# Twelve gates as Strassen pairs, convolution projections inside attention, and the projections in a third plan

## The chip, the core and the metric

The kernel runs on one core of one Trainium2 chip. Time is device time in microseconds (us) of one launch. Each kernel is run several times on the chip, and the median is given; a profile is taken of one execution. Engines: PE (TensorE) does matmuls, ACT (ScalarE), DVE (VectorE) and POOL (GpSimd) do elementwise work, SP (SyncE) issues most DMAs.

## What is computed

One decoder block over 1024 tokens with 16 learned tokens in front. The input is normalised and projected to eight groups of 1024 channels. A gated short convolution and stick-breaking attention run on them side by side, each is projected again and weighted by a sigmoid gate; the sum is projected, normalised and added. A gated MLP with a convolution follows. Cut to what the change touches:

```python
    h = xn @ w_in
    b_c, c_c, h_c, q, k, v, g_conv, g_attn = jnp.split(h, list(splits), axis=-1)
    y_conv = b_c * causal_dwconv(c_c * h_c, conv_w_mix)
    branch_conv = y_conv @ w_proj_conv
    o = stick_breaking_attention(q.reshape(hd), k.reshape(hd), v.reshape(hd))
    branch_attn = o.reshape(bsz, seq_len, D_ATTN) @ w_proj_attn
    gate_conv = jax.nn.sigmoid(g_conv + b_gate[0])
    gate_attn = jax.nn.sigmoid(g_attn + b_gate[1])
    merged = gate_conv * branch_conv + gate_attn * branch_attn
    return merged @ w_out
```

Attention of one head takes, for each block of queries, the scores z, `sigmoid(-z)` (the chance that the stick doesn't break there), a running product of it from the newest key back, and the product of the result with differences of v.

## The kernel before

All float32 matmuls are done in three: each operand is split into a high part (rounded to float32r, a cast on ACT) and a low part (a subtraction on DVE or POOL), and high x high, high x low and low x high are summed in PSUM. 1026 columns (tokens) are kept of the 1040, in three chunks of 342 (`CH`).

A **plain block** makes 128 output channels: 8 row blocks of 128 inputs x 3 chunks x 3 matmuls, 72 matmuls of 342 columns (`plain`, `plain_step`, L356 to L358; in the later stage `Dense.run`, L256 to L258). A **Strassen pair** makes two blocks of 128 channels at once from seven products, each over half of the inputs and half of the tokens: 14 x 12 = 168 matmuls of 260 columns (`strassen_pair`, L807 to L810). It needs sums and differences of the weights (DVE, POOL), and of the tokens (`tops`, made once).

The stages that the change touches, in order of time:

1. **First stage** (`Plan` number one). xnT, the normalised input with channels on the partitions, high and low, stays in memory. Six blocks of q, k and v and one gate, the early one, are plain; the other 42 blocks (c, h, b of the convolution, then q, k, v) are 21 Strassen pairs. Their results are worked on (convolution, splits) and stored to DRAM: y_d, qh_d, ql_d, kh_d, kl_d, vv_d. A further plain gate, the bridge, closes the stage while the first head is loaded.
2. **Attention** (`Plan` number two). 16 heads (8 pairs p, two halves h), each in three units g. Per unit: scores on PE (z, L991 and L992), sigmoid on ACT (fl, L997), scan on DVE (fl, L1008), transposes on PE (tp, L1027), a cast on ACT (ah, L1032) and a subtraction on DVE (al, L458), then the product with v on PE (av, L1042 and L1043), two copies on ACT (L1065, L1068) and an add on POOL (L1072). After both halves POOL adds `ends` (L1085) and the 128 rows go to o_d. Twelve plain gates (`mid_gates`) are mixed in as fillers for PE; ACT evacuates them with Sigmoid (L682), and the gate goes to DRAM (gc_d, ga_d).
3. **Projections** (class `Dense`, in program order). Two late gates; eight blocks with w_proj_conv on y (loaded and split into yT by `load_split`), times the gate, to m_d (`item_pc`); eight blocks with w_proj_attn on the attention result (oT), times the gate, plus m_d (`item_pa`), to mb and mm_d. w_out is split meanwhile into w_o.
4. Output product (po, L1276 to L1278), normalisation, up-projection, down-projection.

In stages 1 and 2 the order on each engine is found ahead of time by class `Plan`: every task has an engine, a cost, a key (the time at which it should run), predecessors, and slots that it takes and frees (buffers, PSUM banks). The planner steps through time, gives each free engine the ready task with the lowest key whose slots are free, and emits it; the instructions of an engine are then held in that order. "ANY" means DVE or POOL, whichever comes first. A task in front that waits on the chip holds up all that stands behind it on its engine. PE thus takes a filler where no attention task is ready.

## Time and profile before

| | |
|---|---|
| median of 3 runs | 1978.43 us (1977.09 to 1979.53) |
| the profiled execution | 1979.65 us, span 1977.8 us |
| mean granted PE clock | 0.993 of full |
| busy: PE, DVE, ACT, POOL | 97%, 58%, 42%, 33% of the span |
| DRAM read, written | 166.02 MB, 70.46 MB |

A row of a group view reads: line, engine, operation, output and inputs, shapes, count, then busy us and mean ns of one, then idle time just before them and what ended it. A row of a window table reads: the window and its length, then for each engine its busy us and, in brackets, its instructions; then PE's granted clock, the share of the DMA engines that was busy, and GB/s. A row of a timeline reads: start, duration, engine, line, operation. PE and DVE instructions overlap at their ends, so a sum of means is somewhat above the busy time.

### The profile page before, as it was taken

What the parts mean: (1) busy time and instruction counts of PE and PEld (TensorE: products, weight loads), DVE (VectorE), ACT (ScalarE), POOL (GpSimd) and SP (SyncE); (2) the same over time, 40 slices, a digit from 0 to 9 for tenths busy, and PEclk for the clock granted to TensorE, in tenths of its full rate; (3) what the DMA queues carried; (4) which work ended last, traced back from release to release, by engine and by line L of the source; (5) the groups of instructions that cost most, each with busy time, mean ns of one, the idle gap of its engine ahead of it and who ended that gap; (6) DMA issues with size and microseconds to landing.
All of it is one profiled execution on the core that took longest, in us unless ns stands there. A gap on an engine that the chain in (4) does not pass through costs nothing.

```text
span 1977.8 us, 32044 instructions
## 1 busy us (share of the span) xinstructions
PE 1918.2 (97%) x12732; PEld 1805.0 (91%) x12732; DVE 1137.9 (58%) x1732; ACT 838.6 (42%) x1766; POOL 647.0 (33%) x484
## 2 busy tenths in 40 slices
PE   6999999999999999999999999889999999999997
PEld 6999999999989999998899999879889988888886
DVE  6836666665457888878331146864544444355547
ACT  5533333344447666767421223544443444321122
POOL 1110000000113232323134631256565555553363
PEclk9999999999999999999999999999999999999999
DMA  3522121454496444542575663221213121353224
GB/s 141 162 80 85 65 79 51 145 151 143 153 236 168 121 142 121 142 120 76 173 215 173 201 175 107 83 86 64 86 65 107 65 85 65 118 168 99 85 86 138
DMA packets 73841, 238.55 MB, mean 121 GB/s; under 512 B 15400, under 2 KB 17224, under 8 KB 72668
## 3 DMA queue, kind: packets, MB, share of 16 engines
q1 hardware_dynamic: 70368, 226.00, 37.6%
q10 hardware_dynamic: 3324, 10.50, 1.7%
q8 instruction: 100, 1.64, 0.3%
q14 instruction: 49, 0.40, 0.1%
HBM read 166.02 MB, written 70.46 MB: 120 GB/s over the span
## 4 chain that ended last, share of the span: by engine, by line
PE 82%; DVE 10%; ACT 2%; DMA 2%; issue 1%; POOL 1%; SPq 0%; ACTq 0%; DVEq 0%; POOLq 0%
PE st L807 7%; PE st L810 7%; PE st L809 7%; PE st L1429 7%; PE st L1431 6%; PE st L1433 6%; DVE fl L1008 4%; PE st L1723 3%; PE st L1721 3%; PE st L1722 3%; PE mm L256 3%; PE mm L257 3%; PE mm L258 3%; PE tp L1027 2%; PE mm L356 2%; PE mm L357 2%
## 5 line engine op out<-in xcount | busy, mean ns | idle before, releaser
L1008 DVE TENSOR_TENSOR_SCAN fl<-fl,upper 114x470 f32<-114x470 f32 (+3 forms) x144 | 208.9, 1466 | 29.9 <-ACT fl L997 29.3
L184 POOL TENSOR_TENSOR a_op<-raw,a_op 128x512 fp32r<-128x512 f32 (+1 forms) x136 | 194.0, 1440 | 88.6 <-ACT a_op L183 85.9
L807 PE MATMUL st<-tT,s_op 128*128 128x260 f32 x672 | 190.9, 284 | 0.0
L809 PE MATMUL st<-tT,s_op 128*128 128x260 f32 x672 | 190.1, 283 | 0.0
L810 PE MATMUL st<-tT,s_op 128*128 128x260 f32 x672 | 190.1, 283 | 0.0
L1429 PE MATMUL st<-opT,a_op 128*128 128x258 f32 (+2 forms) x528 | 171.3, 324 | 4.1 <-ACT snap L1444 1.9
L1431 PE MATMUL st<-opT,a_op 128*128 128x258 f32 (+2 forms) x528 | 169.3, 321 | 2.0 <-DVE opT L184 1.1
L1433 PE MATMUL st<-opT,a_op 128*128 128x258 f32 (+2 forms) x528 | 169.3, 321 | 0.0
L458 DVE TENSOR_TENSOR al<-tp,ah 114x342 fp32r<-114x342 f32 (+3 forms) x288 | 116.9, 442 | 62.5 <-ACT ah L1032 61.7
L183 ACT CAST a_op<-raw 128x512 fp32r<-128x512 f32 (+1 forms) x136 | 85.0, 634 | 155.8 <-DMA raw<-in_w_up_gate_dram 52.4
L1728 DVE TENSOR_TENSOR acc<-acc,st 128x512 f32<-128x512 f32 x144 | 98.5, 687 | 91.1 <-PE st L1723 91.1
L807 PE MATMUL st<-xnT,s_op 128*128 128x260 f32 x504 | 142.5, 283 | 0.0
L1032 ACT CAST ah<-tp 114x342 fp32r<-114x342 f32 (+3 forms) x288 | 106.5, 405 | 84.5 <-PE tp L1027 78.2
L810 PE MATMUL st<-xnT,s_op 128*128 128x260 f32 x504 | 142.3, 282 | 0.0
L809 PE MATMUL st<-xnT,s_op 128*128 128x260 f32 x504 | 141.9, 282 | 0.0
L187 DVE TENSOR_TENSOR raw<-raw 128x512 f32<-128x512 f32 x76 | 76.7, 1009 | 109.0 <-POOL a_op L184 107.0
L1072 POOL TENSOR_TENSOR ot<-ot,half 64x342 f32<-64x342 f32 x48 | 60.3, 1256 | 233.7 <-ACT ot L1068 233.6
L763 ACT CAST s_op<-raw 128x512 fp32r<-128x512 f32 x126 | 77.8, 621 | 124.1 <-PE st L810 116.1
L1431 PE MATMUL st<-opB,a_op 128*128 128x512 f32 (+2 forms) x396 | 127.4, 322 | 1.9 <-DVE opB L184 1.9
L1429 PE MATMUL st<-opB,a_op 128*128 128x512 f32 (+2 forms) x396 | 127.2, 321 | 0.0
L810 PEld LDWEIGHTS st<-tT,s_op 128*128 128x128 f32 x672 | 126.9, 189 | 0.0
L1433 PE MATMUL st<-opB,a_op 128*128 128x512 f32 (+2 forms) x396 | 126.8, 320 | 0.0
(221 smaller groups left out, 5891.0 us busy)
## 6 DMA issues: line engine op xcount, KB each, us to landing
raw<-in_w_in_dram SPq DMA_DIRECT2D x64, 512.0 KB, 3.4
raw<-in_w_up_gate_dram SPq DMA_DIRECT2D x44, 512.0 KB, 3.7
act_d<-owork SPq DMA_DIRECT2D x22, 512.0 KB, 4.2
araw<-act_d SPq DMA_DIRECT2D x22, 512.0 KB
raw<-in_w_down_dram SPq DMA_DIRECT2D x22, 512.0 KB, 3.6
qh<-qh_d SPq DMA_DIRECT2D x32, 256.5 KB, 5.9
ql<-ql_d SPq DMA_DIRECT2D x32, 256.5 KB, 6.6
vv_d<-vt SPq DMA_DIRECT2D x16, 512.0 KB, 3.6
```

The costliest lines, as they stand in the source:

```text
L183: nc.scalar.copy(hi, src)
L184: (lo_engine or nc.vector).tensor_tensor(lo, src, hi.bitcast(F32), op=ALU.subtract)
L458: eng.tensor_tensor(out, src, hi.bitcast(F32), op=ALU.subtract)
L807: nc.tensor.matmul(ps, wt[:, 0, c], xh, start=start and kb == 0, stop=False, skip_group_check=True)
L809: nc.tensor.matmul(ps, wt[:, 0, c], xl, start=False, stop=False, skip_group_check=True)
L810: nc.tensor.matmul(ps, wt[:, 1, c], xh, start=False, stop=kb == 3, skip_group_check=True)
L1008: nc.vector.tensor_tensor_scan(fl[:, ::-1], fl[:, ::-1], upper[:, NT - nk:][:, ::-1], 1.0, op0=ALU.mult, op1=ALU.max)
L1032: nc.scalar.copy(kst["ah"][:n, off:], kst["tp"][:n, off:CH])
L1429: nc.tensor.matmul(ps, wt[:, 0, k], xh, start=start and kb == 0, stop=False, skip_group_check=True)
L1431: nc.tensor.matmul(ps, wt[:, 0, k], xl, start=False, stop=False, skip_group_check=True)
L1433: nc.tensor.matmul(ps, wt[:, 1, k], xh, start=False, stop=stop and kb == 3, skip_group_check=True)
L1728: nc.vector.tensor_tensor(a, a, ps, op=ALU.add)
```

## The change

- Twelve of the 16 gates become six Strassen pairs at the end of the first stage. `done_gate` applies the Sigmoid in one ACT pass over 1026 columns and stores the gate.
- The attention stage gets two plain gates and six of the eight convolution projections as fillers. When the two gates have read xnT for the last time, its memory becomes yT (tag "xy"), and `split_rows` loads the eight row blocks of y into it in place and splits them. The projections' chunks are evacuated on DVE, times the gate (`conv_item`).
- Attention rows 0 to 5 are loaded and split during attention or right behind it into tiles that heads no longer use (`open_qk`, `open_vv`, `both_spare`); rows 6 and 7 into new tiles at the start of the third plan. The store of the last pair's rows is issued by ACT's queue, the others by SP's.
- The class `Dense` is gone. The last two convolution projections and the eight attention projections are tasks of a third `Plan`, which also loads and splits w_out (into the memory of yT once it is free). Most elementwise work there that was fixed to POOL or DVE is "ANY" now, and the order of each engine is held as in the other plans.
- Some later tiles change between the left and the right side of the memory.

```diff
-    xnT = xnt_pool.tile([P, 2, KB, NT], F32R, name="xnT")
+    xnT = xnt_pool.tile([P, 2, KB, NT], F32R, name="xnT", tag="xy")
-    gates = [(1, ob) for ob in range(8)] + [(0, ob) for ob in range(8)]
-    N_FIRST, N_LATE = 1, 2
-    early_gate, bridge_gate = gates[0], gates[1]
-    mid_gates = gates[2:16 - N_LATE]
-    late_gates = [ob for _, ob in gates[16 - N_LATE:]]
-
-    def load_raw(o):
+    gates = [(1, 0)] + [(0, ob) for ob in range(8)] + [(1, ob) for ob in range(1, 8)]
+    early_gate, bridge_gate, mid_gates = gates[0], gates[13], gates[14:]
+    N_LATE = 2
...
+    def plain(o, chunks, key, evac, finish, psum, first_chunk=0, given=None, w=w_in, src=src_x,
+              ready=(), eng="ANY", by="ACT", lead=16.0, space=("wk",), after=()):
+        st = raw_weights(o, w, key - lead) if given is None else given
+        if "hi" not in st and "los" not in st:
+            split_weights(st, key, eng)
+        los = st["los"]
+        before, evacs, banks = None, [], {}
...
+                                  (before, los[kb // 4] if los else None, ready[kb] if ready else None),
+                                  at, (plan_bank,) if kb == 0 else ())
+            evacs.append(plan.add(by, (act_cost if by == "ACT" else dve_cost)(n),
+                                  lambda ci=ci, a=a, n=n: evac(a, n, banks[ci], ci == first_chunk),
+                                  (before, *evacs[-1:], *after), at - 4,
+                                  space if ci == first_chunk and first_chunk == 0 else (), (plan_bank,)))
-        finish(evacs[-1:], at)
+        finish(evacs, at)
...
+    def done_gate(which):
+        def done(ob, u, after, key):
+            t = plan.add("ACT", act_cost(NQ), lambda: nc.scalar.activation(
+                u()[:, T0:], u()[:, T0:], AF.Sigmoid, bias=bias_gate(which, ob)), tuple(after), key + 3)
+            plan.add("SP", dma_cost(NQ), lambda: nc.sync.dma_start(
+                (gc_d, ga_d)[which][ob * P:(ob + 1) * P, :], u()[:, T0:]), (t,), key + 4, (), ("wk",))
+        return done
...
+    blocks += [(48 + 8 * which + ob, ob, done_gate(which)) for which, ob in gates[1:13]]
...
+    nxt = [split_weights(raw_weights(48 + 8 * which + ob, w_in, at - 20.0), at, "ANY")]
+    which, ob = mid_gates[1]
+    nxt.append(raw_weights(48 + 8 * which + ob, w_in, at))
...
-    plan = Plan({"raw": 2, "whi": 1, "wlo": 1, "mm": 2, "z": 2, "tp": 3, "av": 1, "qk": 2, "vv": 1,
+    plan = Plan({"raw": 1, "whi": 1, "wlo": 1, "mm": 2, "z": 2, "tp": 3, "av": 1, "qk": 2, "vv": 1,
...
-    whole_time = len(mid_gates) * item + 250.0
+    fillers = len(mid_gates) + KB - N_LATE
+    whole_time = fillers * item + 250.0
...
         fin = plan.add("POOL", pool_cost(NQ), last_add, tuple(ot_parts), t_o + 1)
-        plan.add("SP", dma_cost(NQ), lambda p=p: nc.sync.dma_start(o_d[p * P:(p + 1) * P, :], out_tiles[p][:, :NQ]),
-                 (fin,), t_o + 1, (), ("ot",))
+        q, cost = (nc.sync, dma_cost(NQ)) if p < NPAIR - 1 else (nc.scalar, 0.15)
+        plan.add("SP" if q is nc.sync else "ACT", cost, lambda p=p, q=q: q.dma_start(
+            o_d[p * P:(p + 1) * P, :], out_tiles[p][:, :NQ]), (fin,), t_o + 1, (), ("ot",))
...
+        evac, finish = gate_out(which, ob, work_tile, ("wk",))
+
+        def ended(evacs, key, finish=finish):
+            mid_last.extend(evacs)
+            finish(evacs, key)
+
+        plain(48 + 8 * which + ob, CH_Q, 20.0 * i, evac, ended, bank_mm, 0, nxt[i],
+              eng="POOL", lead=34.0)
+    def split_rows(kb, parts, src_d, key, after, begin=None, takes=()):
+        def load():
+            if begin is not None:
+                begin()
+            nc.sync.dma_start(parts()[1].bitcast(F32), src_d[kb * P:(kb + 1) * P, :])
+
+        def high():
+            nc.scalar.copy(parts()[0], parts()[1].bitcast(F32))
+
+        def lower(e):
+            hi, lo = parts()
+            low(engine_of(e), lo, lo.bitcast(F32), hi)
+
+        t = plan.add("SP", dma_cost(NQ), load, after, key, takes)
+        t = plan.add("ACT", act_cost(NQ), high, (t,), key)
+        return plan.add("ANY", any_cost(NQ), lower, (t,), key)
...
+    def open_y():
+        t = xnt_pool.tile([P, 2, KB, NT], F32R, name="yT", tag="xy")
+        for kb in range(KB):
+            feats["y", kb] = t[:, 0, kb, :NQ], t[:, 1, kb, :NQ]
...
+    def conv_item(ob, key, tile_of, psum, ready, given=None):
+        u = {}
...
+            g = u["g"][:, a:a + n]
+            nc.vector.tensor_tensor(g, g, ps, op=ALU.mult)
...
+        ld = plan.add("SP", dma_cost(NQ), load, (), key - 8, ("wk",))
+        plain(ob, CH3, key, evac, finish, psum, 0, given, w_proj_conv, src_of("y"), ready, "POOL", "DVE",
+              34.0, (), (ld,))
+    y_open = plan.add(None, 0.0, open_y, tuple(mid_last))
+    y_ready = [split_rows(kb, lambda kb=kb: feats["y", kb], y_d, 24.0 + 2.5 * kb, (y_open,))
+               for kb in range(KB)]
+    late_from = whole_time + 10.0
+    for ob in range(KB - N_LATE):
+        conv_item(ob, 50.0 + (whole_time - 30.0) * ob / (KB - N_LATE), work_tile, bank_mm, y_ready)
+    nxt = [split_weights(raw_weights(KB - N_LATE, w_proj_conv, late_from - 30.0), late_from, "POOL")]
+    nxt.append(raw_weights(KB - N_LATE + 1, w_proj_conv, late_from - 10.0))
...
+    for kb, begin, slot, at in ((0, open_qk, "qk", last_head), (1, open_vv, "vv", last_head + 1),
+                                (2, open_qk, "qk", last_head + 20), (4, open_qk, "qk", late_from),
+                                (5, open_vv, "vv", late_from + 1)):
+        o_ready[kb] = split_rows(kb, lambda kb=kb: feats["o", kb], o_d, at, (), begin(kb), (slot,))
...
-    items = [item_gate(0, ob) for ob in late_gates]
-    n_gates = len(items)
-    dense = Dense(psB0.enter_context(pool("ps_mmB", 3, space=PSUM)), items)
...
-    items += [item_pc(ob) for ob in range(8)] + [item_pa(ob) for ob in range(8)]
-    k = 0
-    for _ in range(24):
-        dense.chunk()
-        if k < 8:
-            load_split(oT, o_d, k)
-            k += 1
...
+    plan = Plan({"raw": 1, "whi": 1, "wlo": 1, "mm": 3, "wk": 2, "ld": 2}, plan)
+    nxt[0]["los"] = nxt[1]["load"] = None
+    o_ready = {kb: split_rows(kb, lambda kb=kb: feats["o", kb], o_d, 2.5 * kb - 15.0, ()) for kb in (6, 7)}
+    o_ready.update((kb, None) for kb in range(6))
+    for i in range(N_LATE):
+        conv_item(KB - N_LATE + i, item * i, lambda: sw_tile("gcl", "wk"), bank_b, (), nxt[i])
...
+    y_users = [t for t in plan.tasks if t.engine == "PE"][-1:]
+    for ob in range(KB):
+        attn_item(ob, item * (N_LATE + ob))
...
+    w_open = plan.add(None, 0.0, open_w, tuple(y_users))
+    for i in range(KB):
...
+        key = item * (N_LATE + 0.85 * i + 0.5)
+        t = plan.add("SP", dma_cost(D), load, (w_open,), key, ("raw",))
+        t = plan.add("ACT", act_cost(D), high, (t,), key + 5)
+        t = plan.add("ANY", any_cost(D), lower, (t,), key + 6)
```

The parts left out move `plain`'s loads into `raw_weights` and `split_weights`, put the attention projections into `attn_item` with the same arithmetic, and open the tiles named above.

More of the change, by code (lines that the diff above doesn't have):

```diff
@@ L914, in block_kernel @@
     at += item
-    nxt = {}
     which, ob = mid_gates[0]
-    def next_load():
-        nxt["raw"] = load_raw(48 + 8 * which + ob)
-    def next_high():
-        nxt["hi"], nxt["lo"] = whole(nxt["raw"])
-        nc.scalar.copy(nxt["hi"], nxt["raw"])
-    ld = plan.add("SP", dma_cost(D), next_load, (), at - 20, ("raw",))
-    h = plan.add("ACT", act_cost(D), next_high, (ld,), at - 10, ("whi", "wlo"))
-    plan.join([plan.add("ANY", any_cost(512),
-                        lambda e, j=j: lo_piece(nxt["raw"], nxt["hi"], nxt["lo"], j, e, 512),
-                        (h,), at - 9) for j in range(2)], ("raw",))
+    nxt = [split_weights(raw_weights(48 + 8 * which + ob, w_in, at - 20.0), at, "ANY")]
+    which, ob = mid_gates[1]
+    nxt.append(raw_weights(48 + 8 * which + ob, w_in, at))
     plan.run()
@@ new lines, in block_kernel, with open_qk, begin, open_vv @@
+    spare = []
+    def open_qk(kb):
+        def begin():
+            tiles = [heads["pool"].tile([P, n], F32R, name=t, tag=t)
+                     for t, n in (("qh", NQ), ("ql", NQ), ("kk", NT))]
+            feats["o", kb] = tiles[0], tiles[1]
+            spare.append(tiles[2][:, :NQ])
+        return begin
+    def open_vv(kb):
+        def begin():
+            v = values_tile().rearrange("p k h d -> p (k h d)")
+            feats["o", kb] = v[:, :NQ], v[:, 1152:1152 + NQ]
+        return begin
@@ L1114, in block_kernel @@
+    m_ctx = ctx.enter_context(ExitStack())
+    mpool = m_ctx.enter_context(pool("mblk", 2, "right"))
     s_ctx = ctx.enter_context(ExitStack())
     sw = s_ctx.enter_context(pool("sw", 2, "right"))
[L1116 to L1125 removed]
@@ L1220, in block_kernel, with bank_b, sw_tile @@
-    for i in range(24):
-        if i % 3 == 0:
-            load_wo(i // 3)
-        dense.chunk()
-        if i % 3 == 1:
-            split_wo(i // 3)
+    def bank_b():
+        return ps_mmB.tile([P, 512], F32, name="mm", tag="mm")
+    def sw_tile(name, tag):
+        return sw.tile([P, NT], F32, name=name, tag=tag)
+    plan = Plan({"raw": 1, "whi": 1, "wlo": 1, "mm": 3, "wk": 2, "ld": 2}, plan)
+    nxt[0]["los"] = nxt[1]["load"] = None
+    o_ready = {kb: split_rows(kb, lambda kb=kb: feats["o", kb], o_d, 2.5 * kb - 15.0, ()) for kb in (6, 7)}
@@ L1226, in block_kernel @@
+    plan.run()
+    pin_to = len(nc.cur_bb.bb.instructions)
     s_ctx.close()
-    slots_de.close()
+    heads_ctx.close()
     psB0.close()
```

352 lines of the change are left out of this document (118 added, 234 removed).

## The prediction

> **What bounds the kernel now.** I read the page's busy shares first, then the chain of waits, then windows by stage, because the mean hides stages with different limits.
>
> ```profile
> span 1977.8 us, 32044 instructions
> PE 1918.2 (97%) x12732; PEld 1805.0 (91%) x12732; DVE 1137.9 (58%) x1732; ACT 838.6 (42%) x1766; POOL 647.0 (33%) x484
> ...
> PE 82%; DVE 10%; ACT 2%; DMA 2%; issue 1%; POOL 1%; SPq 0%; ACTq 0%; DVEq 0%; POOLq 0%
> ```
>
> TensorE (PE) is the bound nearly everywhere; the chain passes through DVE for 10%, part of it in attention. The change touches three stretches, so I cut the span there: a steady piece of the first stage, attention, the gap behind it, and the projections.
>
> ```profile
> core 0: us, PE busy (x) PEld busy (x) DVE busy (x) ACT busy (x) POOL busy (x), PEclk, DMA share, GB/s
> 150.00:200.00 50.00, 50.00 (x420) 50.00 (x419) 33.00 (x48) 20.19 (x42) 2.58 (x2) 1.00 0.24 75
> 551.00:948.00 397.00, 385.07 (x2657) 364.11 (x2657) 312.14 (x432) 260.99 (x672) 111.99 (x84) 1.00 0.51 135
> 970.00:985.00 15.00, 11.80 (x52) 10.58 (x51) 7.40 (x16) 7.49 (x17) 2.77 (x4) 0.77 0.88 287
> 985.00:1155.00 170.00, 170.00 (x1087) 170.00 (x1086) 38.91 (x84) 35.60 (x62) 79.97 (x91) 1.00 0.66 197
> ...
> 551.00:948.00 397.00, 172.16 (x877) 139.69 (x878) 0.00 (x0) 19.68 (x36) 1.00 0.51 135
> ```
>
> The last row is the same window for the projection tiles (mm) alone. Four boundaries come from the timeline and the tile view of po:
>
> ```profile
> 551.47 0.22 PE L991 MATMUL z<-kk,qh 128*114 128x128 f32 x1
> ...
> 947.49 0.22 PE L1042 MATMUL av<-ah,vv 114*128 114x114 f32 x1
> 947.60 0.32 PE L1043 MATMUL av<-al,vv 114*128 114x114 f32 x1
> ...
> L1276 PE MATMUL po<-w_o,mb x216: 314/319/396, 1156.3 to 1262.7; 128*114 128x342 f32 x72, 128*114 128x340 f32 x36
> ```
>
> Attention runs from 551.5 to 947.9, 396.4 us; the projections end at 1156.3, 208.4 us later. In attention PE is 97% busy and DVE 79%; 877 of the 2657 matmuls are fillers, so PE is the bound only because gates are mixed in.
>
> **The first stage: plus 120.0 us.** A Strassen pair is 14 products of 12 matmuls, 168. The steady piece does 420 in 50 us, 119.0 ns each: 20.0 us a pair, six pairs 120.0. Two plain blocks are 144 matmuls at 170 / 1087 = 156.4 ns, 22.5 us. So the move saves 2.5 us of PE a pair, 15 in all. The pairs' other work (weight splits, two Sigmoid passes over 1026 columns) has cover: DVE is busy 33 of 50 us there and ACT 20, and PE never stops. Without that cover a Sigmoid would cost about what an ACT pass over 1026 columns does, quoted below, 1.2 us. Between full cover and 12 of those, I take nothing.
>
> **The projections: minus 95.8 us.** Behind the last av matmul only 720 matmuls remain before the output product: two convolution blocks and eight attention blocks, 720 x 156.4 ns = 112.6 us against 208.4. This also removes the stall behind attention: in the 15 us from 970 PE did 52 matmuls where 96 fit, at a granted clock of 0.77, because it waited for rows of y. Now y is long loaded; attention rows 6 and 7 take its place as the late input. Behind the last av stand two ACT copies, two POOL adds, the store (on ACT's queue, so ACT waits for POOL with the splits of row 5 and of the second convolution block's weights behind it), a load and a split. SP's queue is not held by that wait. By these rows the weights are split about 9 us behind the last av, row 7 about 15 (a load like the store's 4.2, a cast and a subtraction behind it):
>
> ```profile
> L1065 ACT COPY half<-av 64x342 f32<-64x342 f32 x48 | 21.1, 440 | 16.3 <-PE av L1043 15.7
> L1072 POOL TENSOR_TENSOR ot<-ot,half 64x342 f32<-64x342 f32 x48 | 60.3, 1256 | 233.7 <-ACT ot L1068 233.6
> L1085 POOL TENSOR_TENSOR ot<-ot,ends 128x1026 f32<-128x1026 f32 x8 | 15.2, 1902 | 0.6
> L380 POOL TENSOR_TENSOR wlo<-raw,whi 128x512 fp32r<-128x512 f32 x22 | 32.9, 1512 | 53.6 <-PE z L992 35.7 <-ACT whi L469 14.5 <-PE tp L1027 3.5
> L557 ACT CAST hi<-su 128x1026 fp32r<-128x1026 f32 x8 | 8.4, 1052 | 5.3 <-DVE su L831 5.2
> L526 ACT ACTIVATE su<-su,par 128x1026 f32<-128x1026 f32 x8 | 9.3, 1157 | 2.6 <-DVE su L523 2.6
> act_d<-owork SPq DMA_DIRECT2D x22, 512.0 KB, 4.2
> ```
>
> The weights are needed after one block (11.3 us), row 7 after two (22.5): I count nothing, at worst 5 us.
>
> **Attention: the term that decides.** Fillers fall from 875 to 576 matmuls, which would shorten a PE-bound stage by 299 x 156.4 ns = 46.8 us. PE's own need becomes 385.1 - 877 x 0.1564 = 247.9, plus 90.1, 338.0. But DVE's need grows: 18 gated evacuations leave ACT for DVE, and seven of the eight y splits fall to DVE.
>
> ```profile
> L1164 DVE TENSOR_TENSOR gcl<-gcl,mm 128x342 f32<-128x342 f32 x24 | 12.1, 509 | 49.6 <-PE mm L258 45.0 <-DMA gcl<-gc_d 4.6
> L458 DVE TENSOR_TENSOR su<-su,hi 128x1026 fp32r<-128x1026 f32 x8 | 9.8, 1226 | 7.8 <-ACT hi L557 7.8
> ```
>
> 18 x 0.509 + 7 x 1.226 = 17.7 us, so DVE needs 312.1 + 17.7 = 329.8. On DVE, inside attention before (al: low half of a transposed block, fl: scan):
>
> ```order
> L1008 SCALAR_TENSOR_TENSOR fl<-fl,upper 114x584
> L458 TENSOR_TENSOR al<-tp,ah 114x342 x2
> L1008 SCALAR_TENSOR_TENSOR fl<-fl,upper 114x698
> L458 TENSOR_TENSOR al<-tp,ah 114x342
> L458 TENSOR_TENSOR al<-tp,ah 114x228
> ```
>
> and now:
>
> ```order
> L900 SCALAR_TENSOR_TENSOR fl<-fl,upper 114x584
> L353 TENSOR_TENSOR al<-tp,ah 114x342
> L1041 TENSOR_TENSOR gt<-gt,mm 128x342
> L353 TENSOR_TENSOR al<-tp,ah 114x342 x2
> L900 SCALAR_TENSOR_TENSOR fl<-fl,upper 114x698
> L353 TENSOR_TENSOR al<-tp,ah 114x342
> ```
>
> An evacuation (gt) now stands between al's, behind PE's last product of its chunk, with al's and scans queued behind it.
>
> On PE, near the end before, late gates (L256 to L258) still filled in:
>
> ```order
> L1042 MATMUL av<-ah,vv 128x342
> L256 MATMUL mm<-xnT,whi 128x342
> L1043 MATMUL av<-al,vv 128x342
> L1027 MATMUL tp<-ident,fl 114x114
> L1042 MATMUL av<-ah,vv 128x342
> L257 MATMUL mm<-xnT,whi 128x342
> ```
>
> and now, the last three fillers:
>
> ```order
> L253 MATMUL mm<-yT,whi 128x342
> L254 MATMUL mm<-yT,whi 128x342
> L255 MATMUL mm<-yT,wlo 128x342
> L934 MATMUL av<-ah,vv 128x342
> L935 MATMUL av<-al,vv 128x342
> L883 MATMUL z<-kk,qh 114x242
> ```
>
> Behind these, 102 of the 576 av, 117 of the 720 transposes and 42 of the 480 z follow with nothing between them: more than two of the 16 heads run bare. How dense DVE gets is read from windows of attention:
>
> ```profile
> 552.00:576.00 24.00, 21.66 (x137) 19.77 (x137) 15.08 (x18) 11.64 (x30) 2.39 (x1) 1.00 1.04 224
> 576.00:936.00 360.00, 352.06 (x2444) 334.21 (x2442) 288.73 (x400) 242.90 (x626) 106.02 (x82) 1.00 0.48 132
> ...
> 564.00:576.00 12.00, 9.66 (x61) 7.83 (x60) 10.58 (x13) 7.72 (x21) 2.39 (x1) 1.00 1.04 199
> 636.00:648.00 12.00, 10.81 (x77) 9.90 (x74) 11.33 (x15) 8.54 (x24) 4.77 (x4) 1.00 0.25 74
> 732.00:744.00 12.00, 11.16 (x79) 10.51 (x78) 11.33 (x14) 8.72 (x25) 5.51 (x4) 1.00 0.15 47
> 924.00:936.00 12.00, 10.20 (x68) 8.45 (x66) 11.83 (x16) 9.52 (x25) 5.01 (x6) 1.00 0.33 111
> 936.00:948.00 12.00, 10.35 (x71) 9.13 (x72) 8.33 (x16) 6.12 (x17) 3.58 (x2) 1.00 0.06 25
> ```
>
> Start (24 us) and end (12 us) hold few scans and stay as they are, with half a us ahead of them. The middle holds 288.7 us of DVE work and gets 17.7 more: 306.4. DVE reaches 94% where it is pressed (11.33 of 12, twice) and 99% at 924, where fillers are nearly absent. At 94% the middle takes 326.0 us and attention 36.5 + 326.0 = 362.5, 33.9 less than before. The bounds: PE's 338.0 plus the 11.9 us it idles today, 350; or 88%, the pressed window at 564, 348.2 + 36.5 = 384.7. I take 94%, as two separate windows show it with PE at 90 and 93%.
>
> Behind the two gates y is loaded into the tile that held xnT, and five attention rows follow near the end: thirteen loads of half a megabyte on SP among the head loads, with the DMA share at 0.51 today. They have room. But PE's queue meets the first convolution matmuls before all rows of y are split, and a late row would block the transposes and scores behind it. Eight loads at the 4.2 us of the store above, one behind the other, take 34 us; the order puts some 55 z, 53 transposes and 40 av between the last gate matmul and the eighth row's, about 20 us on PE and 25 at DVE's pace. So the delay lies between nothing and 9 us; loads overlap, so I take nothing and keep 9 for the rivals.
>
> POOL's work there stays near 112 us: 14 weight pieces and six row splits, each as long as two pieces, for 30 pieces. But it meets denser scans:
>
> ```profile
> 560.94 1.38 DVE L1008 TENSOR_TENSOR_SCAN fl<-fl,upper 114x584 f32<-114x584 f32 x1 [1.64 <-ACT fl L997]
> ...
> 635.30 2.47 DVE L1008 TENSOR_TENSOR_SCAN fl<-fl,upper 114x584 f32<-114x584 f32 x1
> ...
> 635.25 3.58 POOL L380 TENSOR_TENSOR wlo<-raw,whi 128x512 fp32r<-128x512 f32 x2 [3.34 <-ACT whi L469]
> ```
>
> The same scan takes 1.38 us alone and 2.47 beside a pair of POOL's pieces. The mean over attention already holds such meetings, so by the rows alone I add nothing. The Trainium skill's page GPSIMD Engine Reference, section 1 Specifications, speaks against that: POOL shares its SBUF interfaces with VectorE, with contention where a DVE instruction has two SBUF inputs, so every meeting with a scan costs. By that rule, as an estimate, 15 pairs with scans on half the time are 8 meetings now, and 13 in a denser DVE at most 13: 5 x 1.1 = 5.5 us more, and the sum below would be -4.2 instead of -9.7. The trace shows the meeting; no run of before shows how many the new order makes.
>
> **The sum.** 120.0 - 95.8 - 33.9 = -9.7 us. Output product, up-projection and down-projection keep their instructions; their tiles change sides of the memory, which I count at nothing (plus or minus 2 us). The profiled execution took 1979.65 us, 1.85 over its span; it would take 1970.0. The median of the runs shown, 1978.43, is 1.2 lower: 1968.7.
>
> **Rivals.**
>
> *PE stays the bound.* DVE packs so well that only today's 11.9 us of PE idle remain: attention 350, 22 us gained, 1956. For it: 924 to 936. Against: bare heads, where the window at 936 keeps DVE at 69% and PE at 86%.
>
> *DVE does not pack: slower.* Place: the ring of transposes, ACT's casts and DVE's al. Its waits today:
>
> ```profile
> DVE al L458 <- ACT ah L1032: 61.7, 66, 3.4
> DVE fl L1008 <- ACT fl L997: 29.3, 31, 9.4
> ```
>
> 91 us of waiting; my forecast leaves DVE about 33. If the order with gt between al's and the bare heads holds DVE at 88%, attention takes 384.7, and the total is 1991. Below 90.2% it is slower by more than 4 us, above 92.4% faster by more than that. For it: the whole middle runs at 80% today. Against: there PE was the limit.
>
> *No change.* What is saved elsewhere goes back in attention: y rows 9 us late, five more meetings of a scan with POOL (2.47 against 1.38 us, 5.5 in all), or DVE at 91.3%, which makes attention 372.2 and the total 1978.4.
>
> **How the numbers follow.** A measurement here can tell 0.2%, 4 us, from no change. Forecast (attention 357 to 368) 0.42, PE-bound 0.16, no change 0.21, DVE not packing 0.17, a loss elsewhere 0.04 (a wait at the projections' start or the out product, 5 to 10 us). Faster is the first two, 0.58; slower 0.21. The forecast's own range is 1963 to 1974; with PE-bound at the low end and most of the no-pack case at the high end, 1956 to 1986 holds 8 in 10.
>
> **What would show it.** First stage: six more pairs at 420 matmuls per 50 us. Attention: about 362 us from first z to last av, DVE above 91%, its waits for ah below 40 us, PE idle some 25 us, most in the last 40 us. Projections: 112 to 113 us with no idle and a clock of 1.00. It is wrong if PE waits for yT, if DVE stays under 90%, or if the second late convolution block waits for its weights.

## The result and the profile after

The changed kernel takes 1966.26 us (median of four runs, 1964.59 to 1968.02), the kernel before beside it 1978.0; the ratio is 0.994, with an interval of 0.9923 to 0.9957. That is faster by 0.6%. The prediction was 1968.7.

The page of the changed kernel's profile:

```profile
span 1966.1 us, 32363 instructions
PE 1909.8 (97%) x12876; PEld 1793.0 (91%) x12876; DVE 1194.9 (61%) x1820; ACT 858.5 (44%) x1786; POOL 600.2 (31%) x404
```

The span is 11.7 us shorter than before. Windows cut it at the same places as the prediction: two pieces of the added Strassen pairs, attention, projections, output product.

```profile
core 0: us, PE busy (x) PEld busy (x) DVE busy (x) ACT busy (x) POOL busy (x), PEclk, DMA share, GB/s
550.00:600.00 50.00, 50.00 (x419) 50.00 (x418) 24.39 (x43) 21.04 (x39) 2.57 (x2) 1.00 0.29 96
600.00:660.00 60.00, 60.00 (x502) 60.00 (x502) 23.66 (x42) 23.71 (x45) 0.00 (x0) 1.00 0.38 106
672.00:1029.00 357.00, 344.61 (x2360) 319.51 (x2359) 318.26 (x457) 253.84 (x651) 119.71 (x76) 0.99 0.57 157
1029.00:1142.00 113.00, 113.00 (x718) 113.00 (x717) 39.43 (x70) 25.27 (x39) 36.15 (x29) 1.00 0.74 217
1142.00:1252.00 110.00, 108.07 (x702) 107.66 (x702) 72.19 (x154) 41.48 (x109) 19.03 (x11) 0.98 0.39 121
```

PE does the new pairs without a pause, and the projections too, at a full clock. Attention runs from the first z (672.3) to the end of the last av (1028.6). In the same steps as the sum of the prediction:

| term | predicted | measured |
|---|---|---|
| first stage, to the first z | +120.0 | 672.3 - 551.5 = +120.8 |
| attention | -33.9 | 356.3 - 396.4 = -40.1 |
| projections | -95.8 | 113.5 - 208.4 = -94.9 |
| output product and all behind it | 0 | 824.0 - 821.5 = +2.5 |
| sum | -9.7 | -11.7 |

Inside attention, the stretch between the first 24 and the last 13 us:

```profile
696.00:744.00 48.00, 44.42 (x294) 40.27 (x293) 41.71 (x58) 37.17 (x86) 9.03 (x7) 1.00 0.73 205
744.00:876.00 132.00, 129.69 (x911) 121.44 (x910) 123.67 (x180) 92.95 (x246) 50.42 (x32) 1.00 0.62 176
876.00:1016.00 140.00, 135.87 (x930) 125.72 (x929) 129.04 (x191) 101.14 (x268) 47.47 (x30) 0.98 0.43 119
```

DVE is busy 294.4 of these 320 us, 92%; over all of attention it is 89% (before 79%), and PE 97% as before. So both are close to full, and this profile alone can't say which of the two sets the time. The groups of DVE, and waits of DVE and PE, in attention (a row of waits reads: who waited for whom, us in total, times, the longest):

```profile
L900 DVE TENSOR_TENSOR_SCAN fl<-fl,upper 114x128 f32<-114x128 f32 (+5 forms) x144 | 203.6, 1431 | 21.2 <-ACT fl L889 20.9
L353 DVE TENSOR_TENSOR al<-tp,ah 114x342 fp32r<-114x342 f32 (+3 forms) x288 | 114.8, 439 | 24.8 <-ACT ah L924 24.1 <-PE av L934 0.3
L1041 DVE TENSOR_TENSOR gt<-gt,mm 128x342 f32<-128x342 f32 x18 | 8.8, 492 | 0.0
L353 DVE TENSOR_TENSOR yT<-yT 128x1026 fp32r<-128x1026 f32 x7 | 8.3, 1205 | 0.0
```

```profile
DVE al L353 <- ACT ah L924: 24.1, 30, 1.8
PEld av L935 <- DVE al L353: 11.2, 27, 1.8
PE av L935 <- DVE al L353: 4.7, 10, 1.6
PE mm L254 <- DVE yT L353: 1.8, 4, 0.6
```

The same two waits of PE and its weight loads for al, before:

```profile
PEld av L1043 <- DVE al L458: 14.4, 20, 1.7
PE av L1043 <- DVE al L458: 8.9, 14, 1.4
```

DVE stands less: its wait for ACT's cast, 61.7 us before, is 24.1. PE doesn't wait longer for al than before, but less. So the waits don't tell either which engine holds attention; the experiments do.

One stall is new, in the output product. A timeline of DVE and one of PE show it:

```profile
1143.32 1.22 DVE L353 TENSOR_TENSOR w_o<-raw,w_o 128x1024 fp32r<-128x1024 f32 x1
1155.47 0.69 DVE L1366 TENSOR_TENSOR tmp<-raw 128x512 f32<-128x512 f32 x1 [8.27 <-DMA raw<-in_w_up_gate_dram]
1158.70 0.50 DVE L1249 TENSOR_TENSOR row<-po,g_post 114x342 f32<-114x342 f32 x1
```

```profile
1159.25 0.41 PE L1241 MATMUL po<-w_o,mb 128*114 128x342 f32 x1 [1.93 <-DVE row L1249]
```

The last piece of w_out is split at 1143 and holds the raw buffer until then. The weights of the up-projection go into this buffer, so their load is issued at 1144.6, behind the first output product (1142.1); before it was issued 8 us ahead of it. DVE, in order, stands before those weights until 1155.5 with the evacuation of po queued behind, and PE runs out of PSUM.

### The profile page after: what moved, and what is told of

Same layout as the page of the kernel before. It is cut to its first block, busy times and chain, and to the rows that moved or that the text cites. A ratio compares the mean times of both kernels' runs of the same rounds, so it can differ in the third digit from the quotient of the medians.

```text
span 1966.1 us, 32363 instructions
## 1 busy us (share of the span) xinstructions
PE 1909.8 (97%) x12876; PEld 1793.0 (91%) x12876; DVE 1194.9 (61%) x1820; ACT 858.5 (44%) x1786; POOL 600.2 (31%) x404
## 5 line engine op out<-in xcount | busy, mean ns | idle before, releaser
L709 PE MATMUL st<-tT,s_op 128*128 128x260 f32 x864 | 245.3, 284 | 0.0
L712 PE MATMUL st<-tT,s_op 128*128 128x260 f32 x864 | 244.4, 283 | 0.0
L711 PE MATMUL st<-tT,s_op 128*128 128x260 f32 x864 | 244.3, 283 | 0.0
L900 DVE TENSOR_TENSOR_SCAN fl<-fl,upper 114x128 f32<-114x128 f32 (+5 forms) x144 | 203.6, 1431 | 21.2 <-ACT fl L889 20.9
L709 PE MATMUL st<-xnT,s_op 128*128 128x260 f32 x648 | 183.1, 283 | 0.0
L712 PE MATMUL st<-xnT,s_op 128*128 128x260 f32 x648 | 182.9, 282 | 0.0
L711 PE MATMUL st<-xnT,s_op 128*128 128x260 f32 x648 | 182.3, 281 | 0.0
L353 DVE TENSOR_TENSOR s_op<-raw,s_op 128x512 fp32r<-128x512 f32 x157 | 109.9, 701 | 105.0 <-ACT s_op L665 104.5
L665 ACT CAST s_op<-raw 128x512 fp32r<-128x512 f32 x162 | 100.2, 621 | 161.4 <-PE st L712 153.0
L712 PEld LDWEIGHTS st<-tT,s_op 128*128 128x128 f32 x864 | 163.1, 189 | 0.0
L711 PEld LDWEIGHTS st<-tT,s_op 128*128 128x128 f32 x864 | 162.7, 188 | 0.0
L709 PEld LDWEIGHTS st<-tT,s_op 128*128 128x128 f32 x864 | 162.5, 188 | 0.0
L187 DVE TENSOR_TENSOR raw<-raw 128x512 f32<-128x512 f32 x86 | 81.9, 952 | 109.7 <-POOL a_op L184 107.5
L353 DVE TENSOR_TENSOR al<-tp,ah 114x342 fp32r<-114x342 f32 (+3 forms) x288 | 114.8, 439 | 24.8 <-ACT ah L924 24.1
L1396 PE MATMUL st<-opB,a_op 128*128 128x512 f32 (+2 forms) x396 | 127.6, 322 | 1.9 <-DVE opB L184 1.7
```

What stands on the lines that cost most here:

```text
L353: eng.tensor_tensor(out, src, hi.bitcast(F32), op=ALU.subtract)
L665: nc.scalar.copy(ops[name][:, 0], src())
L709: nc.tensor.matmul(ps, wt[:, 0, c], xh, start=start and kb == 0, stop=False, skip_group_check=True)
L711: nc.tensor.matmul(ps, wt[:, 0, c], xl, start=False, stop=False, skip_group_check=True)
L712: nc.tensor.matmul(ps, wt[:, 1, c], xh, start=False, stop=kb == 3, skip_group_check=True)
L900: nc.vector.tensor_tensor_scan(fl[:, ::-1], fl[:, ::-1], upper[:, NT - nk:][:, ::-1], 1.0, op0=ALU.mult, op1=ALU.max)
```

## Experiments

Times in this part are of attention, from first z to the last av, in the profiled run. Half-heads are the 16 (pair, half) units, each timed from the last av of the one before to its own last av. The kernel before took 1981.7 to 1982.7 us beside these runs; comparisons are by ratio to it.

### The changed kernel once more

> The changed kernel once more, unedited, beside the next two on the same chip: all theories say a ratio of 0.994 to the kernel before, and a profile like the first.

Ratio 0.9930 (0.9915 to 0.9944), attention 356.3 us, and every half-head within 0.1 us of the first profile. So differences in attention well above that are due to the edits. The output product repeats less well: 110.4 us from its first to its last matmul in the first profile, 109.6 in this one.

### Fewer and more fillers

Four, or one, convolution blocks left for the third plan instead of two:

```diff
-    N_LATE = 2
+    N_LATE = 4
...
```

> Edit: four instead of two convolution projections are left for the third plan, so attention has six fillers (two gates, four convolution blocks) instead of eight. Nothing is left out; total PE work is the same. Theory DVE (attention is paced by DVE and its ring): DVE loses only six evacuations of 0.49 us, attention stays near 353 us, projections grow by 22.5 to 136, and the time is about 1985. Rival PE (PE is the bound in attention as before): attention falls by 2 x 11.26 = 22.5 to about 334, projections grow by the same, and the time stays near 1966.

Ratio 1.0062 (1.0047 to 1.0077). Attention took 363.7 us, 7.4 longer, though PE had 144 matmuls (22.5 us) less to do.

```profile
673.00:1036.00 363.00, 332.36 (x2205) 300.98 (x2205) 319.98 (x451) 252.10 (x648) 107.77 (x72) 0.97 0.55 144
...
936.00:984.00 48.00, 39.38 (x252) 32.95 (x253) 45.48 (x62) 34.08 (x91) 11.97 (x9) 0.96 0.45 113
984.00:996.00 12.00, 9.29 (x49) 8.60 (x48) 11.37 (x16) 6.74 (x16) 3.67 (x3) 0.74 0.01 2
```

The fillers run out in half-head 11, before 935, and five half-heads are bare. There DVE is busy 45.5 of 48 us and PE 39.4, and behind that the clock falls. So PE is not the bound with six fillers. This is the side of theory DVE, but 11 us above its 353: DVE is as busy as with eight fillers, 320.0 us, and why attention got longer is not shown.

```diff
-    N_LATE = 2
+    N_LATE = 1
...
```

> Edit: one instead of two convolution projections is left for the third plan, so attention has nine fillers instead of eight. Nothing is left out. Theory DVE: attention grows by three evacuations, to about 358, projections fall by 11.3 to 102.2, and the time is 1957 plus what the shorter cover costs: attention row 7, about 15 us behind the last av, is now needed after one block (11.3), so 4 us, 1961. Rival PE: attention grows by 11.3 to 367.6, and the time is 1966 to 1970.

Ratio 0.9993 (0.9981 to 1.0004): attention 377.7 us, 10 us above the rival PE and 20 above theory DVE. Neither expected it.

```profile
673.00:1050.00 377.00, 355.26 (x2423) 334.40 (x2422) 331.85 (x459) 254.12 (x651) 113.41 (x79) 0.97 0.59 152
```

```profile
L900 DVE TENSOR_TENSOR_SCAN fl<-fl,upper 114x470 f32<-114x470 f32 (+4 forms) x144 | 213.9, 1509 | 21.4 <-ACT fl L889 19.6 <-DMA ga_d<-vv 1.6
```

DVE's work grew by 13.6 us, where three evacuations are 1.5: the same 144 scans took 213.9 us instead of 203.6, and PE stopped for 3.82 us once and for 1.0 to 2.5 us five times. The new number of fillers gave another order on every engine.

Ten Strassen gates instead of twelve, so four gates and six convolution blocks as fillers, with y due later:

```diff
-    early_gate, bridge_gate, mid_gates = gates[0], gates[13], gates[14:]
+    early_gate, bridge_gate, mid_gates = gates[0], gates[11], gates[12:]
...
-    blocks += [(48 + 8 * which + ob, ob, done_gate(which)) for which, ob in gates[1:13]]
+    blocks += [(48 + 8 * which + ob, ob, done_gate(which)) for which, ob in gates[1:11]]
...
-    y_ready = [split_rows(kb, lambda kb=kb: feats["y", kb], y_d, 24.0 + 2.5 * kb, (y_open,))
+    y_ready = [split_rows(kb, lambda kb=kb: feats["y", kb], y_d, 64.0 + 2.5 * kb, (y_open,))
...
```

> Edit: ten instead of twelve gates are made in Strassen pairs; attention has four gates and six convolution blocks as fillers, ten instead of eight. y is due 40 us later and the convolution fillers start later. Nothing is left out. One pair less takes 20.0 us from the first stage. Theory DVE: the two gates are evacuated by ACT, so DVE needs nothing more: attention stays at 356 to 362, and the time is 1946 to 1952. Rival PE: attention grows by 22.5 to 379 and the time is about 1969.

Ratio 0.9974 (0.9964 to 0.9984). Attention took 380.4 us, 24 more, as the rival PE said (+22.5); what lies behind the output product was 3 us longer than in the changed kernel (716.6 for 713.6, or 714.3 in its second profile), which the total shows too.

```profile
652.00:1033.00 381.00, 364.86 (x2504) 342.70 (x2503) 327.32 (x459) 260.65 (x659) 108.67 (x78) 0.99 0.57 152
```

So two fillers more cost about their PE time, and two fewer save nothing. Of the numbers tried, eight gives the shortest attention. As each number also gave another order, and nine fillers took nearly as long as ten, these three runs alone don't show that eight is the corner.

### Less work for DVE

Two runs were to take work off DVE alone. In the first, ACT evacuates the six convolution blocks:

```diff
-            nc.vector.tensor_tensor(g, g, ps, op=ALU.mult)
+            if ready:
+                nc.scalar.copy(g, ps)
+            else:
+                nc.vector.tensor_tensor(g, g, ps, op=ALU.mult)
...
```

> Edit: the six convolution blocks inside attention are evacuated by a plain ACT copy. This leaves out their multiplication by the gate (so m holds the ungated block). DVE loses 18 evacuations of 0.49 us, 8.8 us of the 318 it is busy in attention; ACT gains as many copies of about 0.37 us, 6.6 us on 254. Theory DVE: attention falls by about 9 us to 347, the time to about 1957. Theory corner (eight fillers put DVE and PE level, as the runs with six and with nine or ten fillers suggest): it falls until PE's need of 338 and its idle and clock losses of about 12 us stop it, to about 350, the time to about 1960. Rival PE: attention stays at 356, the time at 1966.

Ratio 0.9965 (0.9953 to 0.9976), attention 365.0 us: 8.7 us longer than in the changed kernel.

```profile
672.00:1037.00 365.00, 344.10 (x2355) 322.87 (x2354) 319.79 (x441) 260.91 (x669) 113.93 (x74) 0.98 0.56 153
```

All three theories said 356 or less. The run doesn't test them, because DVE lost nothing: it is busy 319.8 us, where it was 318.3 without the edit. The planner, which saw room on DVE, gave it two row splits that POOL had (2.4 us), the scans became longer (208.4 against 203.6 us), and the fillers were used up one half-head earlier, so three half-heads were bare and took 58.9 us, where the same three took 52.1. ACT's copies took 0.46 us each, not 0.37.

The second run therefore leaves the planner alone. The costs that it plans with stay; the scan itself covers half of its columns:

```diff
-                        nc.vector.tensor_tensor_scan(fl[:, ::-1], fl[:, ::-1], upper[:, NT - nk:][:, ::-1],
+                        nc.vector.tensor_tensor_scan(fl[:, nk // 2:][:, ::-1], fl[:, nk // 2:][:, ::-1], upper[:, NT - nk + nk // 2:][:, ::-1],
```

> Edit: each scan of attention runs over the newer half of its columns only. This leaves out the running product over the older half. The planner's costs are untouched, so every engine's instructions stand in the same order as in the changed kernel, PE's and ACT's work is the same, and DVE alone loses some 90 of its 318 us. Theory DVE (with eight fillers DVE and its ring set the time of attention): attention falls until PE stops it, its need of 338 plus the few us of waits for y at the start: 343 to 347, the clock stays at 1.00, the time falls by 10 to 13 us, ratio about 0.988. Rival PE (PE has no idle in half-heads 6 to 13, so it is the bound there, and only the two bare half-heads gain): 350 to 353, ratio about 0.991. Rival ring (it is the length of the loop from transpose to cast to low part to product that counts, not DVE's load): 356, ratio 0.993.

Ratio 0.9879 (0.9859 to 0.9900), 1955.78 us, attention 343.9 us: theory DVE, inside its range of 343 to 347. Its window, its scans, and its waits:

```profile
672.00:1016.00 344.00, 335.28 (x2355) 315.74 (x2355) 239.72 (x457) 252.83 (x651) 92.93 (x76) 1.00 0.60 162
```

```profile
L900 DVE TENSOR_TENSOR_SCAN fl<-fl,upper 114x64 f32<-114x64 f32 (+5 forms) x144 | 115.9, 821 | 28.0 <-ACT fl L889 24.9 <-DMA ql<-ql_d 2.3
```

```profile
DVE al L353 <- ACT ah L924: 78.5, 96, 2.2
PEld av L935 <- DVE al L353: 4.2, 13, 0.9
PE av L935 <- DVE al L353: 0.6, 1, 0.6
```

With 78.5 us taken off DVE and no instruction of any engine moved, attention falls by 12.5 us and then stops, at PE's need of 338 and 5.9 us more. So with eight fillers DVE holds attention 12.5 us above what PE allows. 4.4 of these lie in the last two half-heads (35.0 to 30.6), 7.7 in half-heads 2 to 14, where PE is hardly idle in the records, and 0.4 in the first. From the changed kernel's window of attention to this one PE's idle time falls by only 3.7 us, from 12.4 to 8.7, and its busy time by 9.3, from 344.6 to 335.3, for the same matmuls: some 3.4 of these were lost to a half clock (last part), and part of the wait shows in the rows of the weight loads, 11.2 us for al in the changed kernel and 4.2 here. The rivals PE (350 to 353) and ring (356) are out as they were put. But a shorter scan also shortens the way from sigmoid to transpose and the time that an al stands behind a scan, so this run doesn't separate DVE's load from the length of the chain through it. In the last two half-heads of the changed kernel DVE is busy 27.5 of 35 us, so there it is not simply full. The next run adds load beside that chain.

### More work for DVE, less for POOL, and the other way round

The low parts of attention rows 0 to 5, five of which POOL made inside attention, four of them in the last two half-heads, go to DVE:

```diff
+        if eng == "DVE":
+            return plan.add("DVE", dve_cost(NQ), lambda: lower("DVE"), (t,), key, port=True)
...
-        o_ready[kb] = split_rows(kb, lambda kb=kb: feats["o", kb], o_d, at, (), begin(kb), (slot,))
+        o_ready[kb] = split_rows(kb, lambda kb=kb: feats["o", kb], o_d, at, (), begin(kb), (slot,), eng="DVE")
...
```

> Edit: the low parts of attention rows 0 to 5 are made on DVE; four of them were on POOL at 2.4 us, beside its adds. Nothing is left out. Theory (POOL crowds the last two heads): POOL is busy 11.85 of 12 us from 996 to 1008 in the changed kernel, its adds take up to 3.6 us instead of 0.8, and through the half buffer and ACT's order the casts come late; with the rows on DVE the last two heads fall from 35.0 to about 32 us, and the time to about 1963. Rival (DVE paces the bare heads): four times 1.2 us more on DVE make them 2 to 5 us longer, the time 1968 to 1971.

Ratio 0.9943 (0.9928 to 0.9958). The last two half-heads took 37.5 us instead of 35.0: the rival, DVE paces the bare half-heads. POOL, though it had been full for 12 us, was not what held them. Attention grew by 4.1 us for 5.9 us of DVE; half-heads 2 to 13 took the same time to 0.1 us, and the last three 55.8 us instead of 52.1. So load alone, beside an untouched chain, costs time there. For half-heads 2 to 14 load and chain are not separated.

```profile
672.00:1032.00 360.00, 344.61 (x2352) 320.50 (x2352) 324.21 (x462) 254.40 (x650) 106.12 (x71) 0.99 0.57 155
```

All low parts of y go to POOL:

```diff
-    y_ready = [split_rows(kb, lambda kb=kb: feats["y", kb], y_d, 24.0 + 2.5 * kb, (y_open,))
+    y_ready = [split_rows(kb, lambda kb=kb: feats["y", kb], y_d, 24.0 + 2.5 * kb, (y_open,), eng="POOL")
...
```

> Edit: all eight low parts of y are made on POOL; seven were on DVE (1.2 us each), POOL needs 2.4 us. Nothing is left out. Theory DVE: 8.4 us leave DVE between 725 and 760, attention falls by 4 to 8 us. Rival (late rows): eight times 2.4 us stand one behind the other on POOL beside the weight pieces, the last row is split some 8 to 10 us later than now, PE's waits for yT rise from 1.8 to 6 to 10 us and attention grows by 3 to 8 us.

Ratio 1.0018 (1.0009 to 1.0028), attention 372.6 us.

```profile
672.00:1045.00 373.00, 347.19 (x2357) 323.62 (x2356) 321.85 (x450) 253.95 (x651) 142.04 (x83) 0.97 0.56 150
```

The direction is the rival's, at twice its price, but not its mechanism: the last row of y was split 6 us later (it began at 746.2 instead of 739.9), yet PE never waited for yT. Theory DVE isn't tested: the y splits left DVE (8.3 us), but its scans, many of them now beside POOL's splits, became 9.4 us longer, and it was busy 321.9 us. PE's longest stop came from DVE's queue:

```profile
744.37 22.96 DVE L900 TENSOR_TENSOR_SCAN fl<-fl,upper 114x812 f32<-114x812 f32 x13
767.25 0.90 DVE L1045 TENSOR_TENSOR gt<-gt,mm 128x342 f32<-128x342 f32 x2
```

```profile
767.79 0.65 PE L253 MATMUL mm<-yT,whi 128*128 128x342 f32 x1 [11.28 <-DVE gt L1045]
```

In this order, evacuations of filler chunks stand behind 13 scans. PE filled its two banks and then waited 11.28 us. So an evacuation on DVE can hold PE, when a row of scans stands ahead of it; in the changed kernel PE never waited for gt.

### Fillers spread to the end

Two ways to give the bare half-heads fillers. First, each of the 18 chunks of convolution fillers is held until the transposes of a given unit, spread evenly:

```diff
+                                   hold[ci] if hold and kb == 0 else None),
...
+                  hold=tuple(turns[(*units[7 + (39 * (3 * ob + c)) // 18], 0)] for c in range(3)))
```

> Edit: each of the 18 chunks of convolution fillers in attention is held until the transposes of a given unit have been issued, with the units spread evenly from the third half-head to the last but one, and inside a chunk the fillers give way to all attention work. The number of fillers is the same, nothing is left out; the last two half-heads, bare now, get some. Theory (bare heads waste PE): of the 35 us of the last two half-heads PE idles 4.9 and loses about 3.4 to a clock of 0.81 and 0.90; with fillers there, the clock stays at 1.00, and with 24 fillers fewer per bare head in the middle, where PE is 97% busy, attention falls by 5 to 8 us to about 350, the time to about 1960. Rival DVE: the middle is paced by DVE (92% and many windows at 100%), so fillers taken from it free nothing, and those put into the last heads cost nothing either: 1966. Rival (weights late): a held chunk keeps its weights and bank longer, the next block's weights come late, PE waits for mm: up to 10 us longer.

Ratio 0.9937 (0.9922 to 0.9951), attention 357.2 us: no gain, as rival DVE said. The last two half-heads, now with 57 filler matmuls, took 36.5 us, 1.5 more than bare, so fillers are nearly free there, and the clock stayed full:

```profile
994.00:1006.00 12.00, 11.88 (x86) 11.23 (x84) 9.60 (x16) 10.59 (x26) 8.39 (x5) 1.00 0.58 175
1006.00:1018.00 12.00, 12.00 (x87) 11.31 (x86) 11.36 (x17) 9.43 (x24) 5.09 (x3) 1.00 0.14 46
```

But the first eight half-heads, with 54 fewer, took 4.9 us longer. Taking fillers from them freed nothing.

Then only the last eight chunks are held:

> Edit: the first ten chunks of convolution fillers go as they do in the changed kernel; only the last eight are held, each until a given unit of half-heads 8 to 15, and give way to attention work. Nothing is left out. In the changed kernel half-heads 9 to 16 take 160.4 us with 189 filler matmuls, all but 12 of them before half-head 14; in the run with all chunks held they take 156.3 with 243. Theory (PE paces the filled half-heads, DVE and its ring the bare ones): 189 fillers spread evenly need 54 x 156 ns = 8.4 us less than 243, so half-heads 9 to 16 take 148 by PE; DVE's need, 18.8 us a half-head less the part of the last that is done ahead, puts a floor near 150: attention 346 to 350, the time 6 to 10 us below the changed kernel's, ratio about 0.990. Rival DVE (DVE paces all of it): 160, no gain. Rival order (any reordering costs a few us, as the run with the ACT evacuation showed): between 156 and 165, ratio 0.992 to 0.997.

Ratio 0.9967 (0.9954 to 0.9979), attention 363.0 us. Half-heads 9 to 16 took 167.3 us where theory said 150 and the changed kernel takes 160.4. This is worse than rival DVE and at the edge of rival order.

```profile
673.00:1036.00 363.00, 346.02 (x2356) 320.84 (x2355) 325.82 (x458) 253.99 (x651) 113.58 (x75) 0.98 0.57 153
```

Again DVE's work differs with the order: 325.8 us against 318.3 for one instruction more. With it go two stops of PE of 1.94 and 1.59 us with a drop of the clock behind each.

### The stall in the output product

The pieces of w_out come earlier, alone and together with the held chunks:

```diff
-        key = item * (N_LATE + 0.85 * i + 0.5)
+        key = item * (N_LATE + 0.65 * i + 0.5)
```

> Edit: the eight pieces of w_out in the third plan are due 0.65 instead of 0.85 of a block apart, so that the last of them, which holds the raw buffer, is split earlier. Nothing is left out. Theory (late buffer): in the changed kernel the last low part of w_o is made at 1143.3 to 1144.5, the load of the first up-projection weights into that buffer is issued behind it, and lands about 1155.4; DVE stands behind it, 1.93 us of PE wait and a clock of 0.82 follow. With the split early enough that load is issued some 10 us sooner, the product window has no idle, the clock stays 1.00, its length falls from 110.1 to about 106.4 us and the time from 1966.3 to about 1962.6. Rival (crowded DMA engines): the load is slow because g_post, g_pre, mm_d and x are read at the same time; then it lands as late as now, and the time stays at 1966.3.

> Edit: the same, with w_out's pieces due 0.65 of a block apart as in the first experiment. Theory: 2 us below the run without it, from the product window (108.4 instead of 110.4). Rival (what is saved there is lost behind, as in the first experiment where the rest grew from 713.6 to 715.4): the same time.

Alone: ratio 0.9927 (0.9912 to 0.9941). The load is issued 8 us ahead of the first product, and the stall at 1157 is gone. The products take 108.4 us, where theory said 106.4 and the changed kernel has 110.4 and 109.6: PE still waits twice near their end (0.56 and 0.84 us). What lies behind them grew to 715.4 us, so the profiled span, 1966.6 us, is no shorter. With the held chunks: 0.9949 (0.9934 to 0.9964) against 0.9967 without, 1972.23 against 1975.91 us on the same chip, and the products fall from 109.8 to 106.6 us, their length before the change; behind them nothing is lost (714.9 us for 715.2). In that run the load of the up-projection weights is issued at 1141.2, 8 us ahead of the first product, and PE has no idle:

```profile
1150.00:1256.00 106.00, 106.00 (x701) 105.89 (x700) 71.13 (x152) 41.17 (x109) 18.61 (x10) 1.00 0.39 120
```

So the late buffer is the cause of the stall: with the load issued earlier, it doesn't come. The rival (it lands as late as before) is out. But the late load took up to 10.8 us from issue to use, where four loads of w_out of the same size took 3.9 in the kernel before, so crowded DMA engines may have lengthened it; no run separates that. On the changed kernel itself a gain isn't shown (its ratio 0.9930 or 0.994, with the edit 0.9927, intervals overlapping). No version tried here beats the changed kernel beyond doubt.

## Why the prediction came out right

**First stage and projections: right as worked out.** The pairs ran at 419 matmuls in 50 us and hid all their elementwise work (+120.8 for +120.0). The projections took 113.5 us for 112.6, clock 1.00, no idle. The two late inputs came about when the prediction said, counted from the last av at 1028.6. POOL and DVE timelines:

```profile
1035.04 2.63 POOL L275 TENSOR_TENSOR wlo<-raw,whi 128x512 fp32r<-128x512 f32 x2 [2.50 <-ACT whi L367]
```

```profile
1044.16 1.39 DVE L353 TENSOR_TENSOR ol<-ol,oh 128x1026 fp32r<-128x1026 f32 x1 [0.84 <-ACT oh L1009]
```

Weights at +9.1 us (said 9, needed at 11.3), row 7 at +16.9 (said 15, needed at 22.5). So the term "nothing, at worst 5" was nothing.

**Attention: the mechanism right, two sizes off.** The prediction took DVE as the limit, above PE's need of 338, and put attention at 362.5. It took 356.3, just under the range of 357 to 368 that the prediction gave this case, and midway between 362.5 and the 350 of the rival "PE stays the bound". The run with half scans shows who holds it: DVE's work accounts for 12.5 us, whether by load or by the chain through it. The rival "PE stays the bound" is refuted by the same run and by the one with six fillers. The step that was off is DVE's need, 329.8 us: it is 318.3, 11.5 less. The scans are 5.3 us shorter in all (208.9 to 203.6), al 2.1 (116.9 to 114.8), evacuations and y splits 17.1 for 17.7, and back-to-back instructions overlap by 3.5 us more (the sum of the groups less the busy time: 13.7 before, 17.2 after). With this need the prediction's own formula gives 350.2. The other size is the share: 92% in the middle, not 94%, which gives 6.1 back. So of the 12 us that the need was too high, half came back through a share that was too high, and 6.2 us were gained beyond the forecast. That two errors offset each other is luck.

The line "DVE above 91%, and wrong if under 90%" was written for all of attention, and there it is 89%; taken at its word that test failed, though DVE is the limit. DVE's share is no sign of the bound at that precision: by the runs, attention with eight fillers is DVE's busy time over 0.89 to 0.90 in five runs (318.3, 319.1, 324.2, 325.3 and 325.8 us for 356.4, 357.2, 360.5, 363.1 and 363.0), whereas the other two with eight fillers, ACT evacuation and y on POOL, are at 0.88 and 0.86 for the reasons given there. "PE idle some 25 us, most in the last 40" was wrong too: 12.4 us in the records, 5.2 in the last 35; in place of idle time PE's rows are longer, 343.9 us for a need of 338.0.

**Rows of y late: right at nothing.** PE waited for them 1.8 us in all; "wrong if PE waits for yT", taken at its word, failed too, at that price. The bound of 9 us was not seen: with all splits on POOL the last row came 6 us later still, and PE's loss came through DVE's queue.

**Contention: real, and cheaper than before.** The 5.5 us of five more meetings didn't come; the scans got shorter. The Trainium skill's page GPSIMD Engine Reference, section 1 Specifications, has DVE instructions with two SBUF inputs contend with POOL. The traces agree. By their records, a scan that overlaps no POOL instruction takes at most 0.04 us more than the shortest of its shape. The 54 scans that overlap one by more than 0.05 us take 10.9 us more in sum in the changed kernel; it was 15.5 us for 47 scans in the kernel before, 22.2 for 48 with nine fillers and 21.3 for 59 with y on POOL. This is nearly all by which the same 144 scans differ between orders (203.5 to 213.9 us). So a price for every meeting was wrong. Whoever begins second pays: the 29 of the 54 scans that began first lost 0.04 us at most, and the 25 that began while a POOL instruction ran lost 10.6 of the 10.9 us. POOL pays likewise: in the kernel before, an add that began 0.05 us behind a scan took 2.95 us, where the shortest took 0.78. That is how the order sets the sum, and not the amount of POOL's work, whose busy time rose from 112 to 119.7 us.

**Nothing for the output product: 3.7 us too little.** This is the "loss elsewhere" in the place named, below its price of 5 to 10. The prediction followed the instructions that were kept, and not the raw buffer that the third plan now holds until its last split. 1.2 us came back behind it. (In the second profile: 2.9 and 0.5.)

**The sum.** +0.8 +0.9 -6.2 +2.5 = -2.0 us against the forecast: the total is right because two terms of large size were, and because what attention gained beyond the forecast was partly lost again in the other three. The first was worked out, the second is luck.

## What to carry to other kernels

Work that fills the gaps of one engine can be taken out until the next engine's need is reached; find that need in windows of the stage, and expect the two limits to meet softly: here 338 us of PE and 318 of DVE made 356, and not the larger of the two. To ask which engine holds a stage whose order is planned, shorten that engine's instructions, leave the planner's costs alone, and see that the engine's busy time fell; an edit that lets it plan anew moves things by up to 10 us and more, more than most of the terms asked about. Follow buffers across a stage's end: the last user of a shared buffer sets when the next stage's loads start.

## What the runs showed of the hardware

PE's granted clock can halve behind a short stop. In the changed kernel PE stops once for more than 1 us in attention (1.59 us, before 1002.2, for al), and then:

```profile
1000.00:1002.00 2.00, 0.44 (x2) 0.19 (x1) 2.00 (x2) 1.50 (x4) 2.00 (x1) 1.00 0.78 259
1003.00:1004.00 1.00, 1.00 (x10) 0.95 (x9) 0.00 (x0) 0.81 (x3) 1.00 (x1) 0.76 0.88 291
1004.00:1005.00 1.00, 0.85 (x3) 0.29 (x1) 0.56 (x2) 1.00 (x4) 1.00 (x2) 0.50 0.19 70
1010.00:1011.00 1.00, 1.00 (x7) 0.97 (x6) 1.00 (x1) 0.70 (x2) 0.00 (x0) 0.82 0.00 0
```

Full clock during the stop, half from 1003.5 to 1010.4: 6.8 us at half the clock, some 3.4 us of PE work. It isn't the length of the stop that decides. With six fillers a stop of 2.12 us (before 744.9) and with the last chunks held one of 1.53 us (before 1008.4) left the clock at 1.00. In all fourteen profiles a stretch at one clock, as recorded, lasts a whole multiple of 3.41 us, save the one in which the profile ends: the clock changes on a grid. In the last 3.41 us ahead of each of the 73 drops PE was busy 59% or less; of the other 7784 pieces of the grid at full clock only 13 were under 58%, the lowest at 48%. The piece with the stop of 1.59 us in the changed kernel, and the one in which the stop of 2.12 us began, which ran across a border of the grid into the next:

```profile
1000.07:1003.48 3.41, 1.67 (x12) 1.42 (x13) 2.60 (x4) 1.73 (x5) 3.41 (x2) 1.00 0.81 241
740.60:744.00 3.40, 1.82 (x9) 1.14 (x9) 3.40 (x2) 1.85 (x5) 2.17 (x1) 1.00 0.33 125
```

In the runs with evenly held chunks and with half scans no stop in attention reached 1 us, and the clock over attention was 1.00. The Trainium skill's page TensorE: Matmul & The Clock Gate, Part 1, gives an idle window of about 3.4 us for the drop to half rate; the traces agree with the length, but by that rule the stop of 1.59 us would have cost nothing, and there they disagree: a piece of the grid that is half busy is enough. Such a stop can take from PE about three times its length. What it cost in time here is not shown, as DVE held those half-heads: with fillers and a full clock they took 36.5 us.

The same scan instructions differ by 5% in sum between orders of the same work, by which of a scan and a POOL instruction begins first; a sum of means taken from one order holds for another to about 10 us in 330.
